# Expert layer of a two-block float32 network: gathering the tokens of a pair of experts as rows and transposing them, scattering behind the next expert's first products, and cutting a side branch into small parts

## The chip, the cores and the metric

The kernel runs on one core of one Trainium2 chip. The metric is the device time of one execution in microseconds (us), lower is better. All data are float32.

## What is computed

Two transformer blocks over 512 latent tokens of 1024 channels. The first block ends in a mixture of 16 experts in which each expert chooses its 64 tokens; the second block has a state-space mixer whose start states come from 256 context tokens. What the change touches is the expert layer, cut down here:

```python
def expert_choice_ffn(h, w_router, w_gate, w_up, w_down):
    cap = EC_FACTOR * N // N_EXPERTS                      # 64 tokens an expert
    aff = jax.nn.softmax((h @ w_router).astype(F32), axis=-1)
    gate, idx = lax.top_k(jnp.swapaxes(aff, 1, 2), cap)
    xg = jax.vmap(lambda hb, ib: hb[ib])(h, idx)
    hid = jax.nn.silu(jnp.einsum('becd,edf->becf', xg, w_gate)) * jnp.einsum('becd,edf->becf', xg, w_up)
    y = jnp.einsum('becf,efd->becd', hid, w_down) * gate[..., None].astype(h.dtype)
    # y is added to the rows idx of the output
```

and, running beside it, the context half of the second block (its keys and values, and the state-space states of 256 context tokens), which needs nothing of the first block.

## The kernel before, in words

`run` issues the program; a scheduler then lays the instructions of each engine in one fixed order, by the program's order and by what it believes to be ready. Around the change two generators run side by side under `weave`: `g_b` (the experts) and `g_c0` (the context branch). Each yields the share of its work that it has put out, and `weave` always continues the one that is behind. `g_b` yields 0.12 once per expert; `late(0.3, c0)` holds the context back by 0.3.

**Weights.** An expert has 12 loads of 2 MB, 128 partitions x 4096 elements: eight of `w_gate` and `w_up` in turn, four of `w_down`, all issued in order on SP. They go into a ring of four buffers (two in tile `l`, one in `base`, one in `wo`). For the first seven loads three more buffers are used, before they are parted into small ones. When the context generator is done, the ring grows by three buffers of tile `b`, which were the context's: in the program before from expert 8 on.

**One expert** (L1660 to L1722). The gate and up products have 64 tokens as the stationary operand and 512 weights moving (`bigbank`, eight products per load, 64 in all; the records of the profile show two for each float32 product). ScalarE takes the silu (L1675), VectorE multiplies (L1676), TensorE transposes the hidden vector eight times (L1682), ScalarE and VectorE copy it out (L393, L395), and 32 products with `w_down` go into one bank (`bank_mm`). VectorE scales the result into the rows `Y` (L1694, L1695).

**One pair of experts** (`pair`, called when the first of the two begins). VectorE builds the one-hot `S` [token, 128 slots] from the chosen slots (L1591). The gathered tokens come out transposed at once: for each of eight channel tiles four products accumulate over the token tiles, with 128 tokens x 128 channels of `xn` stationary and 128 columns of `S` moving, 32 products of 128x128. ScalarE and VectorE scale them into `XG` (L1600, L1602). Half of the gather goes ahead of the first expert's products, half behind its second load of four. GpSimd multiplies `S` with the affinities (L1604), and four transposes give `P` (L1607). Behind the second expert of the pair eight products `P` x `Y` of 128x512 scatter the rows (`bank_mm<-b`), and VectorE adds each to the running sum (L1720).

**Context** (`g_c0`, `bank_c`, one PSUM bank). Twenty blocks of weights, 512 KB each, issued on ScalarE's queue; per block eight products of 128x256, a three-tap convolution on ScalarE and VectorE (L1760 to L1762), two transposes one step later, copied by ScalarE (L1843), and per group of five blocks four states of 128x512 with copies and sums on ScalarE, GpSimd and VectorE (L393, L1848, L1859, L1860).

PSUM in this stage: two `big` tiles of two banks, three `mm` banks, one `c0` bank.

Of the kernel before, what the change touches and what calls it, by code (L numbers as in the profile page):

```python
# [11 lines left out]
# ---------------------------------------------------------------- host layout  # L12
# [11 lines left out]
def _pack_cols(inp):  # L24
# [31 lines left out]
def _na_bias(rpb):  # L56
    rpb = np.asarray(rpb)[0]                          # [4, 15, 31]
# [14 lines left out]
    return np.ascontiguousarray(np.stack(out, 1).astype(F))      # [128, 12, 256]  # L72


def _consts():
# [3 lines left out]
    ang = np.concatenate([(t // 64)[:, None] * inv, (t % 64)[:, None] * inv], 1)    # [512, 16]  # L79
    cs = np.stack([np.cos(ang), np.sin(ang)], 1)                                    # [512, 2, 16]  # L80
# [23 lines left out]
    ang = np.stack([(t // 64)[:, None] * inv, (t % 64)[:, None] * inv], 1)          # [512, 2, 16]  # L104
    cs = np.stack([np.cos(ang), np.sin(ang)], 1)                                    # [512, 2, 2, 16]
# [26 lines left out]
class Arena:  # L132
    """SBUF of one core as a free list over one tile: alloc and free in program order."""
# [34 lines left out]
class Duo:  # L168
    """Two arenas as one."""
# [10 lines left out]
class Pool:  # L180
    """SBUF whose pieces are tiles of their own, all released together."""
# [12 lines left out]
class Buf:  # L194
    """A piece of an arena or a tile of a pool, seen as [128, *shape]."""
# [31 lines left out]
class Part(Buf):  # L227
    """A piece of a buffer."""
# [9 lines left out]
class Ring:  # L238
    """n equal buffers taken in turn."""
# [15 lines left out]
class Bag:  # L255
    """Equal buffers, given out and taken back; the one that came back first goes out first."""
# [12 lines left out]
    # buffers for a while, until shed  # L269
# [14 lines left out]
class Split:  # L284
    """A block of weights as two exact parts: part i of tile kt along the contraction."""
# [13 lines left out]
def weave(*gens):  # L299
    """Runs generators side by side; each yields the work it has put out, as a part of all of its own."""  # L300
# [9 lines left out]
def ranked(tc, gen, off):  # L310
    """gen's pieces, issued as if they stood off instructions further on."""
# [15 lines left out]

def beside(main, total, fill):
    """main's pieces, which yield total, and fill's, which yield 1, at the same pace."""
# [13 lines left out]
def filled(tc, main, fill):  # L343
    """main's pieces; each yields how much of fill goes in behind it, and maybe the instruction it stays behind."""
# [14 lines left out]
class KA:  # L359
# [5 lines left out]
    # ---------------------------------------------------------------- helpers  # L365
# [48 lines left out]
    # ---------------------------------------------------------------- set up  # L414
    def setup(self, cx):
# [14 lines left out]
        self.m2c_b = Buf(M, [4, 8, 2])                  # sh1, sc1, sh2, sc2 of the second block  # L430
        self.ab2_b = Buf(M, [3, 8])                     # norm gains: block 1 lat, ctx; block 2
# [12 lines left out]
    # a stage's SBUF as a free list  # L444
# [10 lines left out]
    # r ** -0.5 * f of a few columns  # L455
# [5 lines left out]
    # silu(c) columns of two vectors as a padded stationary [128, 8, 32]  # L461
# [9 lines left out]
    # one 512-wide block of the modulation row: [128, 512] with 4 partial sums at partitions 0/1 + 32 j  # L471
# [10 lines left out]
    # modulation vector j (0..5) as columns [128, 8, 2 (lat, ctx)]  # L482
# [11 lines left out]
    # the same with channel 8 p + kt at [p, kt]  # L494
# [11 lines left out]
    # modulation vector j of the latent rows on all partitions [128, 1024]  # L506
# [11 lines left out]
    # x [128, nt, 1024] -> x * rstd in out  # L518
# [12 lines left out]
    # hT [128, 8, nt*128] = xn^T * a + b  # L531
# [13 lines left out]
    # log(1 + exp(z)) of z (destroyed), any sign  # L545
# [16 lines left out]
    # ---------------------------------------------------------------- first block: inputs and modulation  # L562
    def a_in(self, P):
# [6 lines left out]
        mc, a1 = Buf(AB, [2, 8, 2]).ap(), Buf(AB, [2, 8]).ap()          # sh1, sc1  # L570
# [42 lines left out]
    # the other modulation vectors, of both blocks  # L613
# [34 lines left out]
    # ---------------------------------------------------------------- projections  # L648
    def chan(self, w, c, lat=True):                     # 128 columns from c as [128, tokens]
# [6 lines left out]
    def tok(self, w, t, lat=True):                      # 256 columns as [128 tokens of tile t, n]  # L656
# [6 lines left out]
    def g_proj(self, P):  # L663
# [14 lines left out]
        # ---- gated delta net: projections, conv, silu, l2norm  # L678
# [4 lines left out]
        def conv(w, c, tile, dst, lat, kind):  # L683
# [67 lines left out]
        # ---- neighbourhood attention  # L751
# [32 lines left out]
        # ---- differential attention, fourier mixing  # L784
# [686 lines left out]
class KB(KA):  # L1471
# [139 lines left out]
    def g_b(self, experts=range(16)):  # L1611
# [30 lines left out]
        for e in experts:  # L1642
# [27 lines left out]
            for _ in prep:  # L1670
                pass
# [1074 lines left out]
```

## Time and profile before

| | |
|---|---|
| median of 3 runs | 3065.87 us (3064.37 to 3069.57) |
| span of the profiled execution | 3070.7 us (no other time is listed for it) |
| TensorE busy | 2908.0 us, 95% |
| VectorE / ScalarE / GpSimd busy | 1341.8 / 911.1 / 631.7 us |
| DMA | 652.01 MB, mean 212 GB/s |

The stage of the experts runs from about 738 to 1784 us of the span. A busy TensorE is not one at its peak, since its records overlap; what holds it back is read from the chain of waits, from the pauses between its pieces, and from the share of time that the 16 DMA engines are busy in a stretch.

### The profile page before, as it was taken

The page shows a single profiled execution, that of the slowest core. Times are in us where ns is not written, and L with a number is a line of the kernel's source. Part 1 is how long each engine was busy: PE and PEld are TensorE (multiplying, and loading weights), DVE is VectorE, ACT ScalarE, POOL GpSimd, SP SyncE. Part 2 cuts the span into 40 slices and gives each one's busy share as a digit, 9 for nine tenths or more (in the row PEclk, how much of TensorE's full clock was granted, in tenths as well). Part 3 has the DMA queues.
Part 4 walks back from the last instruction along what each step waited for, and adds up shares of the span by engine and source line. Part 5 has one row for each costly group of instructions (what it writes and reads, how often), then busy time and mean ns, then how long its engine had stood idle before and what let it go on. Part 6 is the DMA issues. An engine that isn't in the chain of part 4 may idle for free.

```text
span 3070.7 us, 42582 instructions
## 1 busy us (share of the span) xinstructions
PE 2908.0 (95%) x17172; PEld 1918.0 (62%) x17172; DVE 1341.8 (44%) x2673; ACT 911.1 (30%) x1855; POOL 631.7 (21%) x662
## 2 busy tenths in 40 slices
PE   7999999998999999899999989999999999999998
PEld 4894557756454544244343358787878778878887
DVE  5522546654221211011011057869696945364445
ACT  5511226532111010000000034445454444253333
POOL 3121225521000000000000023323232323242232
PEclk8999999999999999999999989999999999999999
DMA  7216660147979797999999943323332275242231
GB/s 261 75 46 200 206 197 23 35 155 290 371 311 386 318 368 321 423 431 430 431 430 431 430 152 102 103 84 100 86 105 82 87 251 174 94 153 96 96 102 57
DMA packets 255428, 652.01 MB, mean 212 GB/s; under 512 B 15672, under 2 KB 168760, under 8 KB 230656
## 3 DMA queue, kind: packets, MB, share of 16 engines
q1 hardware_dynamic: 212368, 600.95, 51.6%
q10 hardware_dynamic: 42864, 48.35, 4.7%
q8 instruction: 135, 2.21, 0.3%
q14 instruction: 61, 0.50, 0.1%
HBM read 627.61 MB, written 21.64 MB: 211 GB/s over the span
## 4 chain that ended last, share of the span: by engine, by line
PE 61%; DVE 8%; DMA 5%; ACT 2%; issue 1%; POOL 1%; POOLq 0%; DVEq 0%; ACTq 0%
PE bank_mm L367 25%; PE bigbank L367 22%; PE bank_pj L367 6%; PE bank_c L367 3%; DMA b<-in_w_down 2%; DMA l<-in_w_up 1%; PE bank_sm L367 1%; PE bank_y L367 1%; DMA wo<-in_w_down 1%; PE bank_mm L2146 1%; DVE mix L2395 1%; DVE base L2391 1%; DVE mix L2394 1%; DVE c L1929 1%; DMA l<-in_w_down 1%
## 5 line engine op out<-in xcount | busy, mean ns | idle before, releaser
L367 PE MATMUL bank_pj<-c,c 128*128 128x512 f32 (+2 forms) x1368 | 317.7, 375 | 0.0
L367 PE MATMUL bank_mm<-c,c 128*128 128x512 f32 (+1 forms) x1608 | 304.4, 347 | 2.5 <-DVE c L1929 1.3
L367 PEld LDWEIGHTS bank_mm<-c,c 128*128 128x128 f32 x1608 | 259.3, 191 | 42.1 <-DVE c L1929 1.7
L367 PEld LDWEIGHTS bank_pj<-c,c 128*128 128x128 f32 (+1 forms) x1368 | 225.1, 188 | 48.3 <-issue 15.4
L367 PE MATMUL bank_mm<-l 128*128 128x128 f32 (+3 forms) x944 | 229.1, 499 | 4.2 <-DVE l L395 2.0
L1928 ACT CAST c<-base 128x1024 fp32r<-128x1024 f32 x147 | 152.8, 1045 | 254.7 <-PE bigbank L367 105.7
L1929 POOL TENSOR_TENSOR c<-base,c 128x1024 fp32r<-128x1024 f32 x47 | 115.7, 2462 | 453.3 <-ACT c L1928 393.5
L367 PEld LDWEIGHTS bank_mm<-l 128*128 128x128 f32 (+2 forms) x944 | 155.6, 246 | 75.3 <-issue 66.6
L367 PE MATMUL bigbank<-l 128*64 128x512 f32 (+1 forms) x864 | 198.1, 586 | 4.5 <-DMA l<-in_w_up 2.8
L1929 DVE TENSOR_TENSOR c<-base,c 128x1024 fp32r<-128x1024 f32 x100 | 134.9, 1351 | 137.6 <-ACT c L1928 132.8
L367 PEld LDWEIGHTS bigbank<-l 128*64 128x64 f32 (+1 forms) x864 | 62.8, 141 | 117.9 <-issue 105.2
L1676 DVE TENSOR_TENSOR b<-l,bigbank 128x512 f32<-128x512 f32 x32 | 20.6, 684 | 255.7 <-PE bigbank L367 225.7
L367 PE MATMUL bank_c<-b 128*128 128x256 f32 (+3 forms) x496 | 119.2, 385 | 12.6 <-ACT b L1843 8.3
L1604 POOL TENSOR_TENSOR l<-l,ab 128x512 f32<-128x512 f32 x8 | 8.4, 1047 | 560.2 <-DVE l L1591 506.7
L367 PEld LDWEIGHTS bank_c<-b 128*128 128x128 f32 (+1 forms) x496 | 80.6, 194 | 54.8 <-issue 30.1
L367 PE MATMUL bigbank<-out,c 128*128 128x512 f32 x480 | 112.5, 394 | 2.4 <-ACT out L2489 1.8
L367 PE MATMUL bank_mm<-h,sp 128*128 128x512 f32 (+3 forms) x544 | 108.3, 388 | 4.2 <-ACT h L606 3.8
L367 PEld LDWEIGHTS bank_dn<-dn 64*64 64x64 f32 x1920 | 74.0, 134 | 56.4 <-issue 39.1
L367 PE MATMUL bigbank<-b,l 128*64 128x512 f32 x480 | 105.7, 593 | 2.3 <-DMA b<-in_w_up 1.2
L367 PEld LDWEIGHTS bigbank<-out,c 128*128 128x128 f32 x480 | 90.9, 190 | 22.9 <-ACT out L2489 2.0
L1600 ACT ACTIVATE l<-bank_mm,ab,ab 128x128 f32<-128x128 f32 x32 | 14.7, 458 | 292.6 <-DVE l L1602 292.4
L367 PEld LDWEIGHTS bank_mm<-h,sp 128*128 128x128 f32 (+1 forms) x544 | 85.9, 186 | 24.7 <-ACT h L606 4.0
(556 smaller groups left out, 5175.0 us busy)
## 6 DMA issues: line engine op xcount, KB each, us to landing
l<-in_w_up SPq DMA_DIRECT2D x25, 2048.0 KB, 10.6
l<-in_w_gate SPq DMA_DIRECT2D x25, 2048.0 KB, 9.6
l<-in_w_down SPq DMA_DIRECT2D x25, 2048.0 KB, 16.2
base<-in_w_in SPq DMA_DIRECT2D x90, 512.0 KB, 3.8
mods<-in_w_mod SPq DMA_DIRECT2D x80, 512.0 KB, 4.6
base<-in_w_up SPq DMA_DIRECT2D x18, 2048.0 KB, 8.6
wo<-in_w_gate SPq DMA_DIRECT2D x18, 2048.0 KB, 10.1
b<-in_w_gate SPq DMA_DIRECT2D x15, 2048.0 KB, 19.5
```

What stands on the lines that cost most here:

```text
L367: self.mm_ins = self.nc.tensor.matmul(out, l, r, start=start, stop=stop).ins
L1600: nc.scalar.activation(XG[:, kt], b[:, kk], AF.Identity, bias=b2[:, kt:kt + 1], scale=a2[:, kt:kt + 1])
L1604: nc.gpsimd.tensor_mul(sc, S, aff[:, :, ee, None].to_broadcast([128, 4, 2, 64]))
L1676: nc.vector.tensor_mul(hid[:, 512 * j:512 * j + 512], s, ac[1][:, j])
L1928: nc.scalar.copy(hi, raw)
L1929: (nc.vector if self.wn % 4 in self.losplit else nc.gpsimd).tensor_sub(lo, raw, hi.bitcast(F32))
L2146: nc.tensor.transpose(tb[:, z], p[:, 128 * (g0 + z):128 * (g0 + z) + 128], self.ident)
L2391: nc.vector.scalar_tensor_tensor(E[:, h], rw[:, h, 0], gc(1, 0, h), E[:, h], op0=OP.subtract, op1=OP.min)
L2394: nc.vector.tensor_scalar(W[:, h], cb[:, c, 0], gc(0, 0, h), None, op0=OP.mult)
L2395: nc.vector.scalar_tensor_tensor(W[:, h], cb[:, c, 1], gc(0, 1, h), W[:, h], op0=OP.mult, op1=OP.add)
```

## The change

Three parts, in the functions `pair`, `g_b` and `g_c0`.

1. For all pairs but the first, `pair` gathers rows: eight products with `S` [128 tokens x 128 slots] stationary and 512 channels of `xn` moving, into a `big` tile; ScalarE and VectorE copy one half each into `Y`, the buffer that later takes the pair's outputs; eight transposes of 128x128 then give what went into `XG` before. It is called behind the silu of the second expert of the pair ahead, and its pieces are put behind that expert's hidden transposes and its `w_down` products. The first pair keeps the old gather, now all of it ahead of the first expert.
2. The eight scatter products of a pair and their sums are put off (`owed`): four behind the next expert's first two loads, four behind its next two. The last pair is as before.
3. `g_b` yields seven small shares per expert, 0.12 together as before, in place of one, the context starts at 0.1 and its shares count 2.2 times; its weights are asked for one block ahead.

```diff
-    def pair(self, pr):
+    def pair(self, pr, Y, straight=False):
...
+        if not straight:
+            b = self.big()
+            for t in range(4):
+                for h in range(2):
+                    self.mm(b[:, 512 * h:512 * h + 512], S[:, t].rearrange("p e s -> p (e s)"), xn[:, t, 512 * h:512 * h + 512], t == 0, t == 3)
+            self.cp(Y[:, 0:512], b[:, 0:512], "a")
+            self.cp(Y[:, 512:1024], b[:, 512:1024], "v")
+            yield
         for k4 in range(2):
             b = self.bank((128, 4, 128))
             for kk in range(4):
-                for t in range(4):
-                    self.mm(b[:, kk], xn[:, t, 4 * k4 + kk::8], S[:, t].rearrange("p e s -> p (e s)"), t == 0, t == 3)
+                if straight:
+                    for t in range(4):
+                        self.mm(b[:, kk], xn[:, t, 4 * k4 + kk::8], S[:, t].rearrange("p e s -> p (e s)"), t == 0, t == 3)
+                else:
+                    nc.tensor.transpose(b[:, kk], Y[:, 4 * k4 + kk::8], self.ident)
...
+            if e == ex[0]:
+                begun = self.pair(e // 2, yr(), True)
+                next(begun)
             if e % 2 == 0:
-                Y = yr()
-                prep = self.pair(e // 2)
-                next(prep)
-                XG, P = self.XG, self.P
+                XG, P, Y = self.nxt
...
+                if owed:
+                    owed.pop(0)()
+                yield 0.018
...
+            prep = iter(())
+            if e % 2 and e != ex[-1]:
+                prep = self.pair(e // 2 + 1, yr())
+                next(prep)
+            yield 0.006
...
+            elif e % 2:
+
+                def add(ts, P=P, Y=Y):
+                    for t in ts:
...
+                owed += [lambda add=add: add((0, 1)), lambda add=add: add((2, 3))]
-            yield 0.12
+            yield 0.024
...
+        def block():
+            ask()
+            return asked.pop(0)
...
-                w = wr()
-                self.c0_ld(w, w2[:, :, ch:ch + 128])
+                w = block()
...
+C0_LATE, C0_PACE = 0.1, 2.2
...
-            weave(self.g_b(), late(0.3, c0))
+            weave(self.g_b(), late(C0_LATE, paced(c0, C0_PACE)))
```

How the order of instructions moves is shown at three places. First TensorE from the end of expert 5 to the middle of expert 6, before (`bigbank<-... 64x512` are gate and up products, `bank_mm<-... 64x512` down products, `bank_c` the context, `bank_mm<-l 128x128` the old gather, `bank_mm<-b 128x512` the scatter):

```order
L367 MATMUL bank_c_8545<-b_6410 128x512
L1682 MATMUL bank_mm<-base_59,b_6410 128x128 x8
L367 MATMUL bank_c_8552<-b_6410 128x512
L367 MATMUL bank_mm<-l_105 64x512 x8
L367 MATMUL bank_c_8555<-b_6410 128x512
L367 MATMUL bank_mm<-base_95,l_105 64x512 x8
L367 MATMUL bank_mm<-wo_6154,l_105 64x512 x8
L367 MATMUL bank_mm<-l_105 64x512 x8
L367 MATMUL bank_mm<-b_6410 128x512 x8
L367 MATMUL bank_mm<-l_105 128x128 x19
L367 MATMUL bigbank<-l_105 64x512 x8
```

The row `bank_c_8555` is the context's last; the scatter and the first 19 gather products stand in one piece between the last `w_down` load and the next expert's first product. The same place in the changed program, in two pieces; the first is the end of expert 5 (`bigbank<-l_105 128x512` is the new gather, L1707 the hidden transposes, L1613 the new transposes of the gathered rows):

```order
L372 MATMUL bigbank<-l_105 128x512 x2
L372 MATMUL bigbank<-l_105 64x512 x8
L372 MATMUL bigbank<-l_105 128x512 x6
L1707 MATMUL bank_mm<-base_59,b_6410 128x128 x8
L372 MATMUL bank_c_8950<-b_6410 128x256 x2
L1613 MATMUL bank_mm<-base_59,b_6410 128x128 x8
L372 MATMUL bank_mm<-l_105 64x512 x8
```

The gather has moved in front of the hidden transposes, two of its products even ahead of the last up load. Then, on TensorE, the end of the same expert and the start of expert 6:

```order
L372 MATMUL bank_mm<-b_6410 128x512 x3
L372 MATMUL bigbank<-l_105 64x512 x8
L372 MATMUL bank_mm<-b_6410 128x512 x3
L372 MATMUL bigbank<-base_95,l_105 64x512 x8
L372 MATMUL bank_mm<-b_6410 128x512 x2
L372 MATMUL bank_c_9032<-b_6410 128x512
L372 MATMUL bigbank<-wo_6154,l_105 64x512 x8
L372 MATMUL bank_c_9035<-b_6410 128x512
L372 MATMUL bank_c_9042<-b_6410 128x512
L372 MATMUL bigbank<-l_105 64x512 x8
L372 MATMUL bank_c_9045<-b_6410 128x512
```

The scatter now lies between the loads of expert 6, and the context's last product, `bank_c_9045`, behind its fourth load: the context ends one expert later than before, not six. Last, SP's queue at the first loads of expert 8, before:

```order
L398 DMA b_6410<-in_w_gate 128x4096
L398 DMA b_6410<-in_w_up 128x4096
L398 DMA b_6410<-in_w_gate 128x4096
L398 DMA l_105<-in_w_up 128x4096
L398 DMA base_95<-in_w_gate 128x4096
```

and in the changed program:

```order
L403 DMA l_105<-in_w_gate 128x4096
L403 DMA base_95<-in_w_up 128x4096
L403 DMA wo_6154<-in_w_gate 128x4096
L403 DMA l_105<-in_w_up 128x4096
L403 DMA l_105<-in_w_gate 128x4096
```

The three buffers of tile `b` join the ring with expert 12 in place of expert 8. At the end of the stage the last `w_down` load goes to `wo` and the third last to `base`, where before `base` took the last one; the next stage's first weights go to `base`.

## Rows read from the trace of the kernel before

**Rows 1.** Busy time by stretch: us, busy (records) of PE, PEld, DVE, ACT, POOL, then PEclk, DMA share, GB/s.
```profile
738.50:877.40 138.90, 131.73 (x587) 64.94 (x588) 25.27 (x67) 19.98 (x41) 4.14 (x4) 0.98 0.88 353
877.40:1035.28 157.88, 150.28 (x634) 71.24 (x633) 29.38 (x56) 19.35 (x39) 11.30 (x11) 1.00 0.90 351
1035.28:1188.06 152.78, 145.74 (x609) 67.27 (x607) 24.44 (x46) 16.35 (x34) 13.34 (x13) 0.99 0.84 332
1188.06:1258.21 70.15, 67.54 (x286) 33.91 (x288) 11.57 (x21) 3.99 (x8) 1.05 (x1) 0.98 0.84 353
...
1315.27:1431.97 116.70, 110.51 (x485) 48.19 (x485) 15.44 (x28) 5.17 (x10) 1.05 (x1) 0.99 1.01 430
...
1666.77:1783.80 117.03, 112.53 (x486) 48.80 (x488) 13.14 (x21) 5.66 (x11) 0.00 (x0) 0.99 0.95 406
```

**Rows 2.** Chain of waits where it first reaches a load: start us, us, what.
```profile
1242.54 15.68 PE bank_mm L367 x64
1258.21 0.02 issue
1258.23 13.62 DMA l<-in_w_up
```

**Rows 3.** Busy time by short stretch, columns as in rows 1.
```profile
880.00:900.00 20.00, 20.00 (x80) 13.05 (x81) 4.95 (x8) 0.91 (x2) 0.00 (x0) 1.00 0.25 93
...
1040.00:1060.00 20.00, 20.00 (x86) 12.86 (x86) 3.18 (x6) 0.92 (x2) 0.00 (x0) 1.00 0.25 93
1196.00:1208.00 12.00, 12.00 (x54) 9.88 (x55) 1.50 (x3) 0.92 (x2) 0.00 (x0) 1.00 0.22 94
```

**Rows 4.** DMA queues, 738.5 to 1258.2 us: packets, MB, share of 16 engines.
```profile
q1 hardware_dynamic: 11983, 169.07, 80.3%
q10 hardware_dynamic: 17971, 10.57, 6.5%
```

**Rows 5.** DMA queue of the weights, 1258.2 to 1777.5 us.
```profile
q1 hardware_dynamic: 15308, 222.89, 100.3%
```

**Rows 6.** PE groups by form, 738 to 1784 us: line, op, shapes, records | busy us, mean ns | idle before.
```profile
L367 PE MATMUL bank_mm<-l 128*128 128x128 f32 x512 | 124.7, 403 | 0.7 <-DVE l L1591 0.7
...
L367 PE MATMUL bank_mm<-b 128*128 128x512 f32 x112 | 49.7, 597 | 3.9 <-DVE b L1694 3.9
...
L1682 PE MATMUL bank_mm<-base,b 128*128 128x128 f32 x128 | 18.1, 284 | 16.7 <-DVE b L1676 16.7
```

**Rows 7.** Chain of waits, end of expert 1 and start of expert 2.
```profile
847.76 1.29 DVE b L1676 x2
...
849.85 0.70 DVE l L395
...
877.40 15.77 PE bank_mm L367 x54
893.17 13.88 PE bigbank L367 x64
907.06 6.39 PE bank_mm L367 x26
```

**Rows 8.** Chain of waits, hidden vector of expert 5.
```profile
1160.49 1.09 ACT l L1675 x2
...
1169.59 1.29 DVE b L1676 x2
```

**Rows 9.** PE's waits, 740 to 1240 us: engine, line, waited for, us in total, times, longest.
```profile
PE bank_c L367 <- ACT b L1843: 8.3, 15, 1.1
PE bank_c L367 <- ACT b L393: 3.6, 5, 0.8
...
PE bank_c L1842 <- DVE b L1762: 1.8, 1, 1.8
PE bank_c L1818 <- DVE b L1762: 1.8, 1, 1.8
```

**Rows 10.** Groups by line, 1000 to 1900 us, VectorE's one-hot and copies.
```profile
L395 DVE COPY l<-bank_mm 128x512 f32<-128x512 f32 x13 | 9.0, 691 | 12.8 <-PE bank_mm L1682 12.8
...
L1591 DVE TENSOR_TENSOR l<-ab,ab 128x128 f32<-128x128 f32 x20 | 5.8, 289 | 96.5 <-PE bank_mm L367 96.1
```

**Rows 11.** Chain of waits behind the last expert.
```profile
1783.81 5.74 DMA base<-in_w_in
```

More of the change, by code (lines that the diff above doesn't have):

```diff
@@ L325, in late, with paced @@
     yield from gen
+def paced(gen, f):
+    for v in gen:
+        yield v * f
 def beside(main, total, fill):
@@ L1638, in fetch @@
                 self.ld(w, src)
-        gt2, ex = self.gt2_b.ap(), list(experts)
+        gt2, ex, owed = self.gt2_b.ap(), list(experts), []
         self.fg_b = self.gt1_b
@@ L1659, in g_b @@
             for q in range(4):
-                if q == 2:
-                    next(prep, None)
                 for m, src in enumerate((g, u)):
@@ L1683, in g_b @@
                 self.cp(hT[:, 4 * j2:4 * j2 + 4], tb)
+            next(prep, None)
             d = I["w_down"][0, e].rearrange("(a p j) n -> p a j n", a=2, j=8)
@@ L1692, in g_b @@
                             self.mm(dn[64 * h:64 * h + 64], hT[:, 4 * q + j, 64 * a:64 * a + 64], w[:, j, 512 * h:512 * h + 512], a + q + j == 0, a == 1 and q == 1 and j == 3)
+                next(prep, None)
+                if a == 0:
+                    yield 0.018
             pp = slice(64 * (e % 2), 64 * (e % 2) + 64)
@@ L1706, in g_b @@
                 self.c_open()
-            if e % 2:
                 for t in range(4):
-                    if e == ex[-1]:
-                        b = on.pop(0) if on else under(t)
-                        for h in range(2):
-                            hs = slice(512 * h, 512 * h + 512)
-                            self.mm(b[:, hs], P[:, 128 * t:128 * t + 128], Y[:, hs], False, True)
-                        self.c_tile(t, b)
-                        continue
-                    for h in range(2):
-                        b = self.bank()
-                        self.mm(b, P[:, 128 * t:128 * t + 128], Y[:, 512 * h:512 * h + 512])
-                        o = acc[:, t, 512 * h:512 * h + 512]
-                        nc.vector.tensor_add(o, o, b)
-            yield 0.12
+                    b = on.pop(0) if on else under(t)
+                    for h in range(2):
+                        hs = slice(512 * h, 512 * h + 512)
+                        self.mm(b[:, hs], P[:, 128 * t:128 * t + 128], Y[:, hs], False, True)
+                    self.c_tile(t, b)
+            elif e % 2:
+                def add(ts, P=P, Y=Y):
+                    for t in ts:
+                        for h in range(2):
+                            b = self.bank()
+                            self.mm(b, P[:, 128 * t:128 * t + 128], Y[:, 512 * h:512 * h + 512])
+                            o = acc[:, t, 512 * h:512 * h + 512]
+                            nc.vector.tensor_add(o, o, b)
+                owed += [lambda add=add: add((0, 1)), lambda add=add: add((2, 3))]
+            yield 0.024
 BF = mybir.dt.bfloat16
@@ L1793, in g_c0, with ask @@
         w2 = self.w2()
-        w = wr()
-        self.c0_ld(w[:, :, :64], w2[:, :, DT0:DT0 + 64])
+        cols = [(DT0, 64)] + [(K0 + 128 * c, 128) for c in range(4)]
+        for gr in range(4):
+            cols += [(XS0 + 512 * gr + 128 * i, 128) for i in range(4)] + [(BM0 + 128 * gr, 128)]
+        asked = []
+        def ask():
+            if cols:
+                o, n = cols.pop(0)
+                asked.append(wr())
+                self.c0_ld(asked[-1][:, :, :n], w2[:, :, o:o + n])
+        def block():
+            ask()
+            return asked.pop(0)
+        ask()
+        w = block()
         b = self.bank((128, 256), "c0")
@@ L1802, in g_c0 @@
         for c in range(4):
-            w = wr()
-            self.c0_ld(w, w2[:, :, K0 + 128 * c:K0 + 128 * c + 128])
+            w = block()
             for t in range(2):
@@ L1868, in g_c0 @@
                 ch = (XS0 + 512 * gr + 128 * i) if i < 4 else (BM0 + 128 * gr)
-                w = wr()
-                self.c0_ld(w, w2[:, :, ch:ch + 128])
+                w = block()
                 b = self.bank((128, 256), "c0")
```

11 lines of the change are left out of this document (6 added, 5 removed).

## The prediction

> **What bounds the kernel now.** I read the busy time by stretch first, since the stage of the experts has to be told apart from the rest. One row covers about one pair of experts [rows 1]. Up to 1258 us the DMA engines are busy 84 to 90% of the time and a pair takes 153 to 158 us; from there on they are full, and a pair takes 116.7 us. So the stage has two parts with two limits. The chain of waits shows the hand-over: up to 1258.21 it is TensorE's pieces end to end, with short pauses, and there for the first time it follows a load [rows 2]. The reader is to see that the same saving on TensorE is worth its full length before 1258 us and nothing behind it.
>
> The DMA queues say the same in numbers. From 738.5 to 1258.2 us the two queues fill 80.3 + 6.5 = 86.8% of the engines' time [rows 4], so they stand idle 0.132 x 519.7 = 69 us. From 1258.2 to 1777.5 us the weights' queue is at 100.3%, 222.89 MB in 519.3 us [rows 5]: a load of 2.097 MB each 4.89 us. The short stretches show where the idle time lies: 0.25 of 880 to 900, 0.25 of 1040 to 1060, 0.22 of 1196 to 1208 us [rows 3], that is 15, 15 and 9 us. Each is the start of a pair. The chain there [rows 7] shows 15.77 us of scatter and gather in one piece at 877.40, in which no weight buffer comes free; the four buffers fill up and the loads stop.
>
> Which part each saving falls into is read from the order of instructions: 1258.21 is the end of expert 6. Experts 0 to 6 are under TensorE's limit, 7 to 15 under the loads'.
>
> **The change part by part.**
>
> *Gather.* The old one is 64 records a pair, 512 records and 124.7 us for eight pairs [rows 6]: 15.6 us a pair. The new one is eight products of 128x512. The scatter has that shape, 112 records and 49.7 us for seven pairs, 7.1 us a pair [rows 6]; the new transposes are like the hidden ones, 18.1 us for 128, so eight are 1.1 us [rows 6]. That is 8.2 for 15.6, 7.4 us saved a pair. Seven pairs change. Three of them, for experts 2, 4 and 6, have their gather before 1258 us: 3 x 7.4 = 22.1 us on the path. The other four, 29 us, lie in the part that waits for loads and count as nothing; there TensorE will only wait longer. The first pair keeps its price, and drawing its second half ahead of the products moves time within TensorE's chain without adding any.
>
> *The hidden vector's pause.* In front of the hidden transposes TensorE waits for VectorE's two products, 1.29 us in experts 1 and 5, and in expert 1 for one copy of 0.70 behind them [rows 7, 8]. Now six of eight gather products stand there in odd experts. Between 0 and 3 x 2.0 us; I take 1.3 each, 3.9 us, for the copy of 0.70 shows in one of the two rows.
>
> *New waits.* The gather's `big` tile is that of the gate products, so its first product waits for the silu, which takes up to 1.09 us in the chain [rows 8]; a context piece lies ahead of it in some experts. The transposes wait for the copies into `Y`, on VectorE up to one copy of 0.69 behind four one-hots of 0.29 [rows 10], 1.9 us, while the hidden transposes hide 1.1. Bounds: 0 to 3 x 3.0 = 9 us. I take 1 us a pair, 3 us, since both have other work ahead of them in the new order; the copies' two engines and their queues are the reason not to take nothing.
>
> *Scatter put off.* The same eight products. Three still stand right behind the last down load, so the pause for the scaled rows stays; five go between the next loads. No TensorE time is saved, and no buffer comes free later in sum: 0.
>
> *Context in small parts.* The same products. The shares ask for a spread over twelve experts, but the order that came out ends it in expert 6 instead of 5, so it stays in TensorE's part and four states move by some loads. 0 in the middle. What it could win or lose are TensorE's waits on its one PSUM bank, 8.3 + 3.6 + 1.8 + 1.8 = 15.5 us in the four largest rows [rows 9]: at best all of it gone, at worst half of it more. Asking for weights earlier is worth 0, as no row of TensorE's waits before 1240 us names the context's loads; on ScalarE, which issues them, the buffer asked for was read two blocks before, so nothing queues behind the request.
>
> *Four buffers until expert 12.* Experts 8 to 11 lose three buffers. In the pair from 1315 to 1432 us, also on four buffers until the loads of expert 8, the engines were full [rows 1]. The piece that frees no buffer is now six gather products (5.3), the transposes (2.2) and copies, some 9.5 us; three loads in flight cover 14.6. Cost 0, and what it costs without this cover is the third rival.
>
> *End of the stage.* The next stage's first weights wait for buffer `base`, 5.74 us behind the last expert [rows 11]. `base` now comes free two down loads earlier. Between 0 and 5.7; I take 1, as the norm of the last tokens runs beside it.
>
> Sum: -22.1 - 3.9 + 3.0 - 1.0 = **-24 us**. The profiled execution has a span of 3070.7 us, 4.8 above the median, so its 3046.7 becomes **3042 us** as a median.
>
> **Rivals.**
>
> *The context's waits go.* Smaller parts leave the single bank time to be copied out. For: the waits are 0.4 to 0.6 us each and a few weight products would cover one. Against: the printed order still groups five and three of a block's eight products as before. It gives -24 - 15.5, 3026 us.
>
> *The loads are the bound here too, and nothing is won.* Place: the stretches up to 1258 us between the gaps. The whole stretch moved 180 MB in 520 us, about 350 GB/s [rows 1, 4]; if beside the context's small packets the loads could come no closer, what TensorE saves would be waited for, and the time is 3066. Against: the same queue ran at 430 GB/s when left alone [rows 1], and the idle 69 us lie in gaps in which no buffer was free, not in slow packets; the saving needs 24 of them. The Trainium skill (DMA: Bandwidth & Descriptors, "Where 436 GB/s comes from") says that for transfers between HBM and SBUF the limit of HBM per core, some 358 GB/s, binds. By that rule the rate could not rise and the change would be worth nothing. The trace disagrees with it at 430 GB/s over 519 us [rows 5], so I leave this rival no more than its rows earn.
>
> *The ring runs dry, and it is slower.* Place: the ends of experts 7, 9 and 11, where the gather stands ahead of four `w_down` loads on four buffers. If the piece without a freed buffer lasts longer than the three loads in flight, 14.6 us, the engines stop as they did at 880 and 1040 us, 15 us each [rows 3]: +45 - 24 = +21, 3087 us. For: the buffers are fewer in just the part that the loads bound. Against: 9.5 us is shorter, and TensorE waits for loads there, so buffers are empty, not full, when the piece begins.
>
> **How the numbers follow.** Forecast 67%, context waits gone 12%, loads the bound 12%, ring dry 7%, 2% for what I don't see. The range reaches from all good ends, -22.1 - 6 - 15.5 - 5.7 = -49, 3017 us, to the saved gather with all new waits and half of the context's waits more, -22.1 + 9 + 7.7 = -5, 3061 us. It leaves out the second and the third rival, 19%. The forecast's own range is 3032 to 3055. Within 0.2%, which is about what a measurement of this kernel can tell from no change, means 3060 to 3072 us. Faster: 95% of the forecast and the first rival, 76%. Same: the second rival and a little of the forecast, 14%. Slower: the third, some of the second and of the unseen, 10%.
>
> **What would show it.** Right: TensorE's chain first meets a load about 24 us earlier, near 1234 us, at the end of expert 6; the DMA engines' idle time before it falls from 69 to about 45 us, with no gap of 15 us left; from there on they are full, and a pair still takes 117 us. The gather costs 7.1 us with eight transposes of 0.14. Wrong: a DMA share below 1 between experts 7 and 12 (third rival); a chain that follows loads before expert 6 (second); a context whose waits on ScalarE sum to less than 8 us (first); or a pause of several us in front of the new gather or its transposes, which would mean that VectorE's one-hots and copies were priced too low.

## The result, and the profile after

| | before | after |
|---|---|---|
| median, runs | 3067.07 us, 4 | 3049.9 us, 4 (3048.2 to 3052.4) |
| profiled execution, span | 3070.7 us | 3047.4 us |
| stage of the experts: first product of the first gather to the last down product | 1047.0 us | 1027.4 us |
| first transposes of expert 6's hidden vector, from the stage's start | 502.5 us | 477.3 us |

The ratio is 0.9944, 95% interval 0.9930 to 0.9958: 17.2 us faster, where 24 were forecast (3042 us, range 3017 to 3061).

The profiled execution shows where. The stage is 19.6 us shorter; its last down products, before and after, on TensorE's timeline:

```profile
1781.88 3.60 PE L367 MATMUL bank_mm<-base,l 128*64 128x512 f32 x16
...
1759.56 3.60 PE L372 MATMUL bank_mm<-wo,l 128*64 128x512 f32 x16
```

From there to the next stage's products it takes 30.0 us for 30.3. The remaining 3.4 of the 23.3 us lie in parts that the change doesn't touch: the stage began 2.7 us earlier, and in the runs below it begins anywhere between 731 and 740 us. So times are judged by the runs, and the place of a gain by the stage alone.

Busy time by stretch in the profile after (columns as in [rows 1]):

```profile
735.80:874.70 138.90, 133.06 (x593) 64.92 (x594) 27.66 (x74) 21.24 (x43) 5.14 (x5) 0.99 0.86 347
874.70:1027.30 152.60, 147.92 (x611) 60.85 (x610) 29.70 (x55) 18.36 (x37) 10.26 (x10) 1.00 0.95 378
1027.30:1185.30 158.00, 148.50 (x614) 61.17 (x613) 30.82 (x58) 18.95 (x40) 10.26 (x10) 1.00 0.92 354
...
1225.05:1344.72 119.67, 104.65 (x444) 35.49 (x444) 16.29 (x28) 5.73 (x11) 1.05 (x1) 1.00 1.00 421
1344.72:1465.34 120.62, 104.65 (x444) 35.49 (x444) 16.30 (x28) 5.74 (x11) 1.05 (x1) 1.00 0.99 419
...
1587.33:1703.60 116.27, 103.87 (x444) 35.70 (x444) 14.44 (x23) 6.22 (x12) 0.00 (x0) 1.00 1.01 431
```

In the second and third stretch the engines move more than in [rows 1], 378 and 354 GB/s for 351 and 332; the first, with the first pair's old gather, has 347 for 353. Behind 1225 us two pairs take 119.7 and 120.6 us where a pair took 116.7 [rows 1], at 421 and 419 GB/s. Those two stretches were not foreseen.

The chain of waits where it first reaches a load, which answers to [rows 2]:

```profile
1214.49 10.54 PE bank_mm L372 x48
1225.05 14.98 DMA wo<-in_w_gate
...
1243.77 15.91 DMA wo<-in_w_gate
```

The hand-over still lies at the end of expert 6, 30.5 us earlier within the stage (489.2 for 519.7). The forecast was 24. TensorE now meets the loads at the third load of expert 7 and not at the fourth, with 166.29 MB moved by 1225 us against 169.07 MB by 1258 [rows 4], 2.8 MB or 6.5 us of loads. The DMA queues of 735.8 to 1225 us and of 1225 to 1744 us:

```profile
q1 hardware_dynamic: 11796, 166.29, 84.1%
q10 hardware_dynamic: 18710, 10.95, 7.1%
...
q1 hardware_dynamic: 15145, 220.60, 100.0%
```

Idle before the hand-over: 0.088 x 489.2 = 43 us for 69 [rows 4]; the forecast was 45. As forecast, no gap of 15 us is left, but the first pair's gather, which kept its products, still costs 13. Behind it 220.60 MB came in 519 us where the rate of [rows 5], 222.89 MB in 519.3, gives 222.8: 2.2 MB, 5 us short.

The gather by form, 735 to 1764 us, seven pairs (columns as in [rows 6]), and the transposes of one in the chain of waits, in expert 3:

```profile
L372 PE MATMUL bigbank<-l 128*128 128x512 f32 x112 | 51.8, 605 | 6.1 <-ACT l L1694 5.9
```

```profile
998.81 0.86 PE bank_c L372 x2
999.68 0.88 PE bank_mm L1613 x8
```

A gather takes 51.8 / 7 = 7.4 us and its eight transposes (L1613) 0.88, as priced (7.1 and 1.1). In front of the transposes there is no pause here, since a context piece stands ahead of them.

PE's waits from 735.8 to 1225 us, which answer to [rows 9]:

```profile
PE bank_c L372 <- ACT b L1889: 6.2, 12, 0.7
PE bank_c L1888 <- DVE b L1794: 3.8, 2, 2.0
PE bank_c L372 <- ACT b L398: 2.9, 4, 0.8
PE bank_mm L1707 <- DVE b L1695: 2.3, 2, 1.5
...
PE bigbank L372 <- ACT l L1694: 1.2, 2, 0.8
```

### The profile page after: what moved, and what is told of

Read it like the earlier page. It is cut to its first block, busy times and chain, and to the rows that moved or that the text cites. A ratio compares the mean times of both kernels' runs of the same rounds, so it can differ in the third digit from the quotient of the medians.

```text
span 3047.4 us, 42013 instructions
## 1 busy us (share of the span) xinstructions
PE 2854.8 (94%) x16892; PEld 1830.5 (60%) x16892; DVE 1347.6 (44%) x2681; ACT 915.1 (30%) x1861; POOL 631.9 (21%) x662
## 4 chain that ended last, share of the span: by engine, by line
PE 60%; DVE 7%; DMA 6%; ACT 1%; issue 1%; POOL 1%; POOLq 0%; DVEq 0%; ACTq 0%; SPq 0%
PE bigbank L372 23%; PE bank_mm L372 22%; PE bank_pj L372 7%; DMA wo<-in_w_gate 3%; PE bank_c L372 3%; PE bank_y L372 1%; PE bank_sm L372 1%; DMA b<-in_w_gate 1%; DMA base<-in_w_gate 1%; DMA wo<-in_w_down 1%; PE bank_mm L2191 1%; DVE base L2436 1%; DVE mix L2440 1%; DVE mix L2439 1%; DVE c L1974 1%
## 5 line engine op out<-in xcount | busy, mean ns | idle before, releaser
L372 PE MATMUL bigbank<-l 128*64 128x512 f32 (+2 forms) x1088 | 273.1, 587 | 23.2 <-DMA l<-in_w_gate 8.6
L1973 ACT CAST c<-base 128x1024 fp32r<-128x1024 f32 x147 | 152.7, 1045 | 254.2 <-PE bigbank L372 105.6
L372 PEld LDWEIGHTS bigbank<-l 128*64 128x64 f32 (+2 forms) x1088 | 90.1, 145 | 189.8 <-issue 155.2
L1694 ACT ACTIVATE l<-bigbank 128x512 f32<-128x512 f32 x32 | 17.4, 594 | 469.5 <-PE bigbank L372 469.5
L372 PE MATMUL bank_mm<-l 128*64 128x512 f32 (+3 forms) x544 | 128.1, 577 | 4.5 <-DMA l<-in_w_down 2.9
L372 PE MATMUL bigbank<-wo,l 128*64 128x512 f32 x448 | 102.0, 597 | 9.2 <-DMA wo<-in_w_gate 9.2
L372 PE MATMUL bigbank<-base,l 128*64 128x512 f32 x432 | 98.4, 597 | 9.9 <-DMA base<-in_w_up 8.7
L372 PE MATMUL bigbank<-c,ffn 128*128 128x512 f32 x432 | 100.3, 390 | 0.0
```

The lines of the kernel that those rows point to most:

```text
L372: self.mm_ins = self.nc.tensor.matmul(out, l, r, start=start, stop=stop).ins
L1694: nc.scalar.activation(s, ac[0][:, j], AF.Silu)
L1973: nc.scalar.copy(hi, raw)
```

## The experiments

All figures of a run's stage come from its one profiled execution, as in the table above; the time is the median of its runs, the ratio is to the kernel before on the same chip. The stage before is 1047.0 us, with expert 6's hidden vector at 502.5. A few us between two single executions need not come from the edit: up to that vector e2 has the same order of TensorE's products as after, and e12 the same as e1, yet after and e12 take 477.3 us, e1 and e2 480.6. The granted clock goes with it. Past the first 20 us it is 1.00 in every stretch of 20 us in after and e12, and e1 has two like these:

```profile
791.25:811.25 20.00, 17.54 (x70) 7.05 (x68) 3.71 (x7) 1.93 (x4) 0.00 (x0) 0.91 1.00 399
...
1031.25:1051.25 20.00, 17.29 (x68) 6.83 (x68) 1.92 (x5) 1.93 (x4) 0.00 (x0) 0.91 0.89 331
```

By an estimate, 9% of twice 20 us, that is 3.6 us, for the 3.3 measured. The expectations below count the stage before as 1045 us and e8's as 1001; to the last down product on TensorE's timeline they are 1047.0 and 1003.6.

| run | time, us | ratio, interval | stage, us | expert 6's hidden vector, us |
|---|---|---|---|---|
| after | 3049.9 | 0.9944 (0.9930 to 0.9958) | 1027.4 | 477.3 |
| e1_seven_buffers | 3045.5 | 0.9931 (0.9919 to 0.9943) | 1024.7 | 480.6 |
| e2_rows_early | 3065.4 | 0.9994 (0.9984 to 1.0004) | 1044.0 | 480.6 |
| e3_rows_late | 3079.2 | 1.0041 (1.0029 to 1.0053) | 1056.5 | 504.0 |
| e4_context_held | 3032.9 | 0.9888 (0.9875 to 0.9901) | 1010.0 | 430.2 |
| e5_products_seven | 3077.9 | 1.0032 (1.0021 to 1.0043) | 1049.1 | 497.0 |
| e6_scatter_at_once | 3054.2 | 0.9953 (0.9941 to 0.9966) | 1032.9 | 477.9 |
| e7_first_pair_rows | 3051.5 | 0.9948 (0.9936 to 0.9961) | 1032.7 | 481.1 |
| e8_context_held_to_8 | 3027.4 | 0.9864 (0.9850 to 0.9878) | 1003.6 | 443.5 |
| e9_held_to_6 | 3043.8 | 0.9918 (0.9905 to 0.9932) | 1023.7 | 480.8 |
| e10_held_first_rows | 3027.8 | 0.9865 (0.9851 to 0.9878) | 1007.5 | 447.2 |
| e11_late_growth | 3020.7 | 0.9850 (0.9837 to 0.9864) | 1000.1 | 439.7 |
| e12_rows_early_seven | 3054.8 | 0.9956 (0.9942 to 0.9969) | 1029.3 | 477.3 |

### Which gathers count: e3, e2, e12

```diff
-                prep = self.pair(e // 2 + 1, yr())
+                prep = self.pair(e // 2 + 1, yr(), e // 2 + 1 <= 3)
```

This is e3; the last argument says which pairs keep the small products. In e2 and e12 it is `e // 2 + 1 > 3`, and e12 also has `C0_LATE, C0_PACE = 0.3, 1.0`.

> The changed kernel with rows and transposes for the gathers of experts 8, 10, 12 and 14 alone; those of experts 2, 4 and 6 are by 64 small products again. Theory (savings count only up to the hand-over): the first part is as long as before, the hand-over comes 20 to 24 us later than in the changed kernel, near 1247 us, the engines stand idle for about 65 us before it, and the time is 3066 to 3075, ratio 1.000 to 1.003. Rival (each gather's saving counts alike): three sevenths of the gain are lost, 3057, ratio 0.9968.

Without the early gathers the stage is 29.1 us longer than after, 26.7 of them ahead of expert 6's hidden vector, as the theory has it; the rival is out. The time, 29.3 us above after, is 4 above the theory's range, which left out the four buffers: from expert 6's to expert 15's hidden vector e3 takes 535.3 us for 527.3 before the change. In short stretches of e3 (columns as in [rows 1]) the loads falter again as in [rows 3], less deep and one expert earlier, at the ends of experts 0, 2 and 4, where the scheduler now puts the small products:

```profile
816.57:836.57 20.00, 20.00 (x90) 13.54 (x91) 9.46 (x34) 4.22 (x8) 0.00 (x0) 1.00 0.75 282
936.57:956.57 20.00, 20.00 (x88) 13.77 (x86) 0.86 (x3) 0.92 (x2) 0.00 (x0) 1.00 0.77 308
1116.57:1136.57 20.00, 20.00 (x88) 11.18 (x87) 3.27 (x8) 1.19 (x3) 0.00 (x0) 1.00 0.59 226
```

> The changed kernel with rows and transposes for the gathers of experts 2, 4 and 6 alone; the four later pairs are gathered by 64 small products again. Theory (savings on TensorE count only up to where the loads take over, near 1225 us): the hand-over comes at 1225 us as in the changed kernel. Behind it each of the four later gathers takes 7 us longer, which TensorE has to spare; only on four buffers, at the ends of experts 7, 9 and 11, may the piece that frees no buffer cost some us each. Time 3050 to 3060, ratio 0.9945 to 0.998. Rival (each gather's saving counts alike): four sevenths of the gain are lost, 3060, and the hand-over shows no change; together with the next run the two tell it apart.

A miss in size: the later gathers' old form costs 16.6 us of stage, 13.2 of them behind expert 6's hidden vector, and 15 us in the runs. The loss lies in three stretches behind the hand-over, at the ends of experts 6, 8 and 10, where the scheduler puts the small products among the down products:

```profile
1239.90:1259.90 20.00, 20.00 (x91) 9.72 (x92) 3.27 (x8) 0.92 (x2) 0.00 (x0) 1.00 0.72 284
...
1359.90:1379.90 20.00, 20.00 (x90) 11.80 (x91) 4.09 (x10) 1.83 (x4) 0.00 (x0) 1.00 0.76 298
1479.90:1499.90 20.00, 20.00 (x88) 12.47 (x86) 4.09 (x10) 1.83 (x4) 0.00 (x0) 1.00 0.81 308
```

TensorE is busy all of each, and the engines stand idle 0.28, 0.24 and 0.19 of 20 us, 14 us together. That is the mechanism of the prediction's third rival, a gather during which a ring of four runs dry, at 4 to 6 us a time for the old gather.

> Rows and transposes for the gathers of experts 2, 4 and 6 alone, as in the run that left the four later pairs to 64 small products, but with the context's buffers in the ring from expert 8 as before. That run lost 15 us against the changed kernel, where the prediction had counted the later gathers as nothing. Theory (they are worth nothing where the ring has seven buffers; on four a gather of 15.7 us stops the loads): no stretch behind the hand-over falls below 0.95 but perhaps the first gather behind it, and the stage is within 3 us of the 1024.7 of the run with seven buffers and rows for all; time 3043 to 3049, ratio 0.992 to 0.994. Rival (the gather's length counts behind the hand-over also on seven buffers): dips of 0.7 to 0.8 as in the run on four, stage 1033 to 1044, time 3053 to 3064, ratio 0.995 to 0.9985.

Neither holds as it stands. The stage, 4.6 us above e1's, lies between the two; the time, 9 above e1, is on the rival's side. Behind expert 6's hidden vector, where the two programs begin to differ, e12 takes 7.9 us more (534.8 for 526.9), and its engines fall at one place, the end of expert 6, where the ring still has four buffers:

```profile
1214.64:1234.64 20.00, 20.00 (x88) 14.38 (x86) 0.82 (x2) 0.92 (x2) 0.00 (x0) 1.00 0.92 382
1234.64:1254.64 20.00, 20.00 (x94) 8.79 (x92) 3.27 (x8) 0.92 (x2) 0.00 (x0) 1.00 0.80 316
```

That is 5.6 us of idle time. Past it every stretch up to the end of the loads is full, so the gathers that do meet seven buffers cost some 2 us together.

### Four buffers or seven: e1

```diff
-C0_LATE, C0_PACE = 0.1, 2.2
+C0_LATE, C0_PACE = 0.3, 1.0
```

> The changed kernel with the context's old pace and start (1 and 0.3 in place of 2.2 and 0.1), so that the three buffers of the context join the ring at expert 8 as before and not at expert 12; TensorE's order of the context's pieces is the same as in the changed kernel. Theory (the ring of four lets the engines run dry at the ends of experts 7 and 9): from 1225 to 1744 us the changed kernel moved 220.6 MB where 430 GB/s would have moved 223.3, 6 us short, in the stretches around 1283 and 1400 us; here these stretches are full and the time is 4 to 7 us below that of the changed kernel, about 3044, ratio to before near 0.9925. Rival (four buffers cost nothing; the dips come from the loads' own order or from the wait for the gather): the dips stay and the time is that of the changed kernel, 3050, ratio 0.9944.

The DMA queue of e1 from 1225 to 1735 us, and a stretch around the gather for expert 8:

```profile
q1 hardware_dynamic: 15057, 219.31, 100.5%
```

```profile
1270.00:1290.00 20.00, 19.06 (x85) 7.92 (x85) 5.07 (x11) 2.98 (x6) 1.05 (x1) 1.00 1.01 431
```

The dips are gone (219.31 MB in 510 us, 430 GB/s). From expert 6's to expert 15's hidden vector the stage takes 526.9 us, as before the change (527.3), for 533.0 after: 6 us, as expected. 3.3 of them were lost again ahead of expert 6 in this execution, with the clock shown above; the runs, 4.4 apart, have intervals that overlap.

What happens on four buffers shows in the changed kernel, on SP's queue and in three stretches of 5 us:

```profile
1270.17 0.33 SPq L403 DMA_DIRECT2D l<-in_w_down  x1
1282.09 0.33 SPq L403 DMA_DIRECT2D l<-in_w_gate  x1
```

```profile
1276.00:1281.00 5.00, 4.07 (x24) 2.06 (x24) 2.88 (x6) 2.49 (x6) 0.00 (x0) 1.00 0.98 419
1281.00:1286.00 5.00, 5.00 (x25) 1.63 (x23) 0.00 (x0) 0.00 (x0) 0.00 (x0) 1.00 0.82 308
...
1401.00:1406.00 5.00, 5.00 (x25) 1.57 (x23) 0.00 (x0) 0.00 (x0) 0.00 (x0) 1.00 0.77 279
```

Silu, hidden vector, gather and transposes free no buffer: 11.9 us between two requests. That is under the 14.6 us of three loads, and yet the engines run dry. The three were asked for at 1258.57, 1263.42 and 1270.17 us and share the engines with what was asked for before them: at 1270.17 the oldest is part way in, and it lands at 1274.85. The gap at 1401 us is as long (1390.37 to 1402.28). By their GB/s the two stretches lose some 3 of the 6 us (308 and 279 for 430); where the rest lies these rows do not show.

### The parts priced at nothing: e5, e6

e5: `self.pair(e // 2 + 1, yr(), True)` for every pair, and `C0_LATE, C0_PACE = 0.3, 1.0`.

> All of the change but its gather and its four buffers: every pair is gathered by 64 small products as before, and the context's buffers join the ring at expert 8 as before; the scatter put off, the context's smaller parts, its weights asked for earlier and the hidden vector's new place stay. Theory (these parts together are worth nothing, as the prediction had each of them): the stage is as long as before, 1045 us from its first gather to its last down product, the time 3064 to 3072, ratio 0.999 to 1.0015. By the sum of the runs so far it should be a little slower: the run with seven buffers has a stage 20.6 us shorter than before, the early gathers alone are worth 24.5 by the run without them, so some 4 us are lost by the rest, 1049 and 3071. Rival (the smaller parts of the context win part of what was gained, as the sum of TensorE's waits on its bank fell): stage 1035 to 1041, ratio 0.996 to 0.9985.

The stage, 1049.1 us, is close to the theory's; the time is slower than the rival's and the theory's, 9 us above before. Its profiled execution was the fastest of eight. So these parts win nothing, and cost 2 us by the stage and 6 to 13 by the interval; what the slower executions lose was not seen. Against e1, which differs in the gathers alone, the stage is 24.5 us longer: 16.4 up to expert 6's hidden vector, where the forecast had 22.1, and 8.1 behind it, where it had nothing. So e5 is 5.5 us ahead of before at that vector (497.0 for 502.5) and loses 7.7 behind it, where the small products for expert 8 now meet four buffers at the end of expert 6 (a DMA share of 0.76 from 1254 to 1274 us).

e6:

```diff
-                owed += [lambda add=add: add((0, 1)), lambda add=add: add((2, 3))]
+                add((0, 1, 2, 3))
```

> The changed kernel with the scatter's eight products at the end of the pair, as before, in place of behind the next expert's first products. Theory (worth nothing): the piece of TensorE that frees no buffer is now the scatter, some 8 us, shorter than the loads in flight; time 3047 to 3053, ratio 0.9935 to 0.9955. Rival (putting it off keeps the buffers coming on the ring of four): dips of 2 to 4 us at the ends of experts 1, 3, 5, 7, 9 and 11, time 3056 to 3066, ratio 0.9965 to 0.9995.

Between the two: 5.5 us of stage, 4 in the runs, with intervals that overlap. Two stretches of e6, where the changed kernel has 0.88 and 0.84:

```profile
1015.40:1035.40 20.00, 20.00 (x76) 7.53 (x76) 6.88 (x10) 0.00 (x0) 0.00 (x0) 1.00 0.71 291
1175.40:1195.40 20.00, 18.82 (x73) 5.91 (x73) 3.55 (x6) 1.17 (x2) 4.13 (x4) 1.00 0.74 302
```

The dips are there; expert 6's hidden vector is only 0.6 us later. Putting the scatter off lets loads go ahead, and they are worth something behind the hand-over.

### Where the context lies: e4, e8, e9

```diff
+def held(k, gen):
+    while True:
+        with k.tc.issue_after(k.mm_ins):
...
+                v = next(gen)
...
-            weave(self.g_b(), late(C0_LATE, paced(c0, C0_PACE)))
+            weave(self.g_b(), late(C0_LATE, paced(held(self, c0), C0_PACE)))
```

`mm_ins` is the last product given out; e8 has `C0_PACE` 1.5, e9 1.1.

> The changed kernel, but each piece of the context's branch is held on TensorE behind the expert's product that precedes it in program order, so that the branch really lies spread over experts 0 to 11; in the changed kernel it ends in expert 6. Theory (the first part is TensorE's, and the engines stand idle for 42 us in it, 13 of them in the first gather): about 30 of the context's 105 us of products leave the first part, the hand-over comes earlier by about as much, at expert 5 or 6, and behind it TensorE has the time to spare; of the idle 42 us some 20 to 25 are won, and up to 5 are given back on the ring of four. Time 3025 to 3038, ratio 0.987 to 0.991. Rival (the first part is bound by the loads, slowed by the context's small packets): the packets are the same wherever they lie, and the time stays at 3050, ratio 0.9944. Second rival (the context's pieces behind the hand-over delay the release of buffers): 3055 or more.

> As the run with the context held, but at a faster pace (1.5 in place of 2.2): its last piece lies in expert 8, and its buffers join the ring four experts earlier. Theory (two costs against each other: each context piece before the hand-over lengthens TensorE's part, and each pair on four buffers costs up to 3 us behind it): some 15 us of products come back into the experts 1 to 6, of which a part is covered, and the dips behind expert 9 go; the stage is 1005 to 1018 us (1010 with the slower pace), time 3028 to 3040, ratio 0.987 to 0.991. Rival (only where the context lies counts): 10 to 15 us longer, 3043 to 3048, ratio 0.992 to 0.9935.

Both as the theory has it, e8 a little better than its range: 17 and 22 us faster than after. In e8 the stretch up to expert 6's hidden vector, 443.5 us, has 76.6 us of context products for 105.2, and TensorE idle for 9.9 us for 22.7: 28.6 and 12.8 us less, of which 7.6 are given back in the busy time of PE's other products, 33.8 in all. Up to expert 15's hidden vector 10 of them go again, 543.0 us for 533.0, where the loads set the pace. The context ran in the part that was short of TensorE, beside a part that has 15 us a pair to spare.

> As the runs with the context held, at a pace of 1.1: its last piece lies in expert 6, as in the changed kernel, so all of its products stay before the hand-over and only their order among the expert's products differs; its buffers join the ring at expert 7 or 8. Theory (TensorE's waits on the context's bank come from pieces that stand too close together, and an even spread takes them away): before the hidden vector of expert 6 TensorE stands idle for some 10 us in place of 22.7, that point lies at 463 to 468 us of the stage in place of 477.3, and the ring of seven gives 6 us more behind it; time 3030 to 3036, ratio 0.9875 to 0.990. Rival (the run held to expert 8 gained only because 28.6 us of products left the first part): the point lies at 475 to 478 us, time 3042 to 3046, ratio 0.992 to 0.9935.

The theory fell. PE's largest waits in e9 up to expert 6, and ScalarE's timeline at one of them:

```profile
PE bigbank L382 <- ACT l L1704: 8.6, 3, 6.2
PE bank_c L382 <- ACT b L408: 5.5, 1, 5.5
```

```profile
1002.15 0.37 ACTq L413 DMA_DIRECT2D b<-in_w_in  x1
1002.63 0.42 ACT L1806 ACTIVATE b<-b 128x256 f32<-128x256 f32 x1 [8.12 <-DMA b<-in_w_in]
```

The waits on the bank fell from 19 to about 7 us, but ScalarE, about to ask for context weights, waited 8.12 us for an earlier load that took 39.83 us in the chain, and TensorE waited for what stood behind that request. TensorE's idle time is 21.9 us for 22.7. The time is e1's, and so is the part behind expert 6's hidden vector (525.8 us for 526.9). So an even spread within the same part wins nothing as it came out here; it is the context's place that e8 moved.

### The first pair, and a version that beats both: e7, e10, e11

e7 and e10 take the first pair's gather as rows (`begun = self.pair(e // 2, yr())`, drawn twice), e7 on the changed kernel, e10 on e8.

> The changed kernel with the first pair gathered as rows and turned too. Theory (TensorE sets the first part): the first gather takes 7.1 us, a copy and 1.1 us of transposes in place of 15.7, so the stage is 5.5 to 7 us shorter and the engines' first gap, 13 us, falls to about 6; time 3043 to 3045, ratio 0.9918 to 0.993. Rival (the loads behind the first gap take what they take, or the wait for the copies eats it): 3048 to 3050, ratio 0.994.

A miss on both sides: the first hidden vector comes 5.5 us earlier (39.5 for 45.0), and by expert 6 it is 3.8 late. TensorE's idle time up to there is 30.2 us for 22.7; the scheduler had put the context's pieces in another order, which e7 does not tell apart from the gather.

> The context held to expert 8, and the first pair gathered as rows too. In the run with the first pair alone 5.5 us were won by the first hidden vector (39.5 us of the stage for 45.0) and 9 lost again by expert 6, with the context's pieces in another order and TensorE's waits on its bank at 24 us for 19. Theory (the loss was the order's, not the gather's): with the order held, the 5 to 7 us stay won up to the hand-over; stage 994 to 997 us for 1001, time 3020 to 3023, ratio 0.984 to 0.9855. Rival (the loads bind there already, since the engines are 96% busy in this version): the gain goes into waits for loads, 3025 to 3028, ratio 0.9862 to 0.987.

> As the run before this one, but the context's buffers join the ring one expert after its last piece is written, not at once. In the run held to expert 8 the first load into such a buffer waited on SP's queue from 1259.95 to 1275.74 us for GpSimd's last use of it, no other load was sent meanwhile, and the engines fell to 0.56 and 0.92 in the two stretches of 20 us there, some 10 us idle. Theory (that wait is the cause): the dip goes, 4 to 9 us less than the run before this one, at most 3 of them given back on the ring of four for one expert more; time 3013 to 3019, ratio 0.982 to 0.9842. Rival (the buffers are full for another reason there): no difference, within 2 us of the run before this one.

e11's edit, beside e10's:

```diff
-            if not self.c0 and len(wr.b) < 7:
+            if not self.c0:
+                gone += 1
+            if gone == 2 and len(wr.b) < 7:
```

e10 shows no gain over e8 in the runs: the rival's time. So the theory about the first pair is neither shown nor refuted.

e11's time, 3020.7 us, is 7 below e10's and 1.7 above its range, but its edit is not shown to be the cause. SP's queue in e8 at the wait that e11 takes away, and in e11 at its longest gap there:

```profile
1259.95 0.33 SPq L413 DMA_DIRECT2D base<-in_w_gate  x1
1275.74 0.33 SPq L413 DMA_DIRECT2D b<-in_w_up  x1
...
1239.33 0.33 SPq L413 DMA_DIRECT2D l<-in_w_down  x1
1254.92 0.33 SPq L413 DMA_DIRECT2D l<-in_w_gate  x1
```

In e8 one load into a buffer that the context hadn't left held up every load behind it for 15.8 us. In e11 that wait is gone, and a gap of 15.6 us stands in its place, where a gather, a context piece and two rounds of transposes meet four buffers:

```profile
1236.97:1256.97 20.00, 19.07 (x86) 10.03 (x84) 7.04 (x14) 4.34 (x9) 2.09 (x2) 1.00 0.59 242
```

From expert 6's to expert 15's hidden vector e11 takes 543.3 us for e10's 543.2. All of the 7.4 us between their stages lie ahead of expert 6 (439.7 for 447.2), where the order of TensorE's products is the same in both. There the granted clock was 1.00 all through in e11, and in e10 it was 0.92 in the first 20 us, in which the first gather took 8.64 us for e11's 7.12, and lower again in two more stretches:

```profile
799.10:839.10 40.00, 34.91 (x144) 13.64 (x146) 9.97 (x31) 6.29 (x11) 0.00 (x0) 0.94 0.96 392
839.10:879.10 40.00, 39.48 (x176) 19.29 (x172) 9.74 (x22) 8.22 (x20) 1.05 (x1) 0.97 0.93 386
```

By time e8, e10 and e11 can't be told apart, as their intervals overlap. At 3020.7 us e11 is 1.5% faster than before and about 1% faster than the changed kernel; what it shows beyond e8 is open.

## Why the prediction was right, point by point

- **Two limits.** Right ahead of the hand-over. TensorE saved 25.2 us up to expert 6's hidden vector (502.5 to 477.3), and e3 gives all of it back (504.0). By an estimate 1.6 of them are the clock's, which was 0.96 from 838.5 to 878.5 us before and 1.00 in the same place after. "Nothing behind it" was too strong, as the next point shows.
- **Gather, -22.1.** Right: busy PE up to that point falls from 478.5 to 454.6 us, and e3 and e5 put the early gathers at 26.7 and 16.4 us there. That the four later ones count as nothing holds only where the ring is deep: on four buffers they are worth 15 us (e2), 8 on a ring that grows at expert 8 (e12, e5), and without the new gather the four buffers would have eaten most of the gain.
- **The hidden vector's pause, -3.9.** Hardly there: L1707 still waits 2.3 us for VectorE, where L1682 waited 3.3 up to 1258 us.
- **New waits, +3.** 1.2 us for the silu (the row of `bigbank <- ACT l L1694`) and none in front of the transposes before the hand-over. This term and the one above it were both too large, and that they cancel to within 1 us is luck.
- **Context in small parts, 0.** Its waits on the bank sum to 19 us as before, so the first rival is out. The two largest rows of [rows 9] give 0.55 and 0.72 us a wait, not 0.4 to 0.6.
- **Scatter put off, 0.** Mis-sized: worth about 4 to 5 us by e6, whose interval overlaps that of after.
- **"Four buffers until expert 12 ... Cost 0".** The step that failed. From expert 6 to expert 15 the stage takes 5.6 us more than before, and e1 takes them away. "Three loads in flight cover 14.6" counted the three as if all were asked for when the piece begins. The pair that was to show that four buffers are enough, 1315 to 1432 us, lies behind the first load into tile `b`, so it had seven:

```profile
1295.33 0.43 SPq L398 DMA_DIRECT2D b<-in_w_gate  x1
```

- **End of the stage, -1.** -0.3: from the last hidden vector to the last down product 17.1 us in both, from there 30.0 for 30.3. The load into `base` is no longer in the chain; VectorE's and ScalarE's work on the last tokens takes nearly as long.

Sum of the profiled execution: -25.2 + 5.6 - 0.3 = -20 us against -24 forecast; the runs say 17.2 (the profiled execution before spans 3070.7 us, above the highest of its listed times, 3069.6). So the number came out within its range with one term at nothing that cost 5.6. The second rival is out: the loads took up all that TensorE saved. The Trainium skill (DMA: Bandwidth & Descriptors, "Where 436 GB/s comes from") gives some 358 GB/s as the limit of HBM per core; no run here agrees, e1's row above being 430 GB/s over 510 us.

## What to carry to other kernels

Split a stage by what ends the waits before pricing an edit: the same 7.4 us were worth about their full length ahead of the hand-over and 2 to 4 us behind it, the less the deeper the ring. Then look for the longest stretch of TensorE's work in which no buffer comes free, and measure it from request to request on the loads' queue, not by the count of loads in flight. Work without a deadline belongs in the part that has time to spare, and a scheduler that knows no such part has to be told. And before an edit gets the credit for a gain, see that the gain lies behind the edit: e11's lay ahead of it.

## What was not expected of the hardware

- A gap of 11.9 us between two requests ran the engines dry twice, with three loads of 4.89 us asked for ahead (0.82 and 0.77 of 5 us); a gap of 15.6 us left 0.59 of 20 us (e11).
- A 512 KB context load, a median of 4.6 us from issue to landing before and 17.7 in the changed kernel, took 39.83 us in e9, and a wait for it on ScalarE's queue reached TensorE.
- Parts that no edit touched moved the stage's start by up to 9 us between executions, more than most of the edits here are worth. Every engine's instructions up to there are the same; the mean granted clock was 0.99 in the earliest (e1, 731.25 us) and 0.97 in the latest (e7, 740.01 us).
